# A planned single-core encoder block: steadier operand order, early weights for one output product, and new first and last transfers

## The chip, the cores and the metric

The kernel runs on one core of one Trainium2 chip, in one launch, without collectives. The metric is device time in microseconds. Three runs of the kernel before stand as its time, and one more execution was recorded by the hardware profiler; every row of the trace comes from that one. Engines are named as in the profile: PE (matmul), PEld (its weight loads), DVE, ACT, POOL, and SP, which only issues transfers.

## What is computed

One pre-norm layer on a float32 input of 512 tokens by 1024 channels. An input projection feeds two attention branches, each is gated, and one output projection and a final norm close the layer. Cut to what matters:

```
h = rmsnorm(x, norm_g)
q_lat, c_kv, k_rope, z_a, q_b, k_b, v_b, z_b, q_idx, k_idx, w_idx, gate_a, gate_b = split(h @ w_in)
y_a = chunk_causal_attention(latent q, latent k and v, 8 heads) * silu(z_a)
score = sum over index heads of relu(q_idx . k_idx) * w_idx        # keep the 128 best keys per query
y_b = attention over the kept keys, with a position bias, 8 heads, * silu(z_b)
merged = sigmoid(gate_a) * (y_a @ w_o_a) + sigmoid(gate_b) * (y_b @ w_o_b)
out = rmsnorm(x + merged @ w_out, final_g)
```

## The kernel before

**Precision.** Every operand of a large matmul is split into a rounded high part and the rest (a low part), each in its own 128x512 tile. ACT makes the high part by a copy (L302) or a scaled copy (L311), DVE or POOL subtracts it to get the low part (L328, L330, L339). A product is then three matmuls, high*high, high*low and low*high (`mm3`, recorded at L400). Transposes through the PE are at L417.

**The planner.** Nothing in the program's order is fixed by loops. Each piece of work is a generator that yields one step at a time (a thread, with a priority and a small random nudge), and the class `Flow` plays the whole kernel through at build time: it holds for each engine when it is free, for each buffer when it was last written and read and by whom, and for transfers a modelled queue. Again and again it picks, among the threads' next steps, the one with the smallest key, emits that instruction, and books its modelled duration. So each engine's instruction order is the order of the planner's picks; on the chip each engine then runs its own list strictly in that order and waits where an operand is not there. The pick is this (L199 onwards):

```
s = self.start(t.req, eng)
key = (s + BIAS * t.prio + t.nudge, t.prio)
```

`start` is the first moment at which the engine is free and every operand and buffer is ready. `DRAW` seeds the nudges, so another number gives another order among near-equal steps.

**Buffers.** 73 slots of 128x512 float32 hold nearly everything; four raw buffers of 128x1024 receive weights; eight PSUM banks are shared out by class.

**Start.** `loads` issues on SP, in this order: the first 128 rows of x transposed (s_x, 256 KB), norm_g, the first kv weights, the second rows of x, and so on. `setup` issues the first index-query weights (s_er<-w_qi, 128 KB) from ACT. POOL loads the identity and the latent gains (`setup_pool`, L431). `early_x` splits x (times norm_g) into s_xg tiles: for the first rows ACT makes the high part in three pieces and DVE one low part over all 512 columns. `early_mm` then runs, for each of the eight row blocks k, 6 matmuls of 384 columns for the index queries and 12 of 328 columns for the kv latent, 18 in all.

**Middle.** Projections, the head-by-head latent attention, the index scores, a top-128 search on DVE (L825, L826), the sparse attention, with projections as filler for the PE. The tanh of the gate projection of branch a (s_sig) is written out to scratch in DRAM by SP (`gate`, bias_scratch<-s_sig, eight times) and read back after the projections.

**Output projection.** It is a seven-product scheme on 2x2 blocks; `output` runs products 1, 7, 2, 6, 5, 4, 3 in this order, each 24 matmuls of 512 columns or the same in halves. Their right operands are sums or differences of blocks of w_out. `out_job` loads the blocks into raw buffers from SP, DVE forms the difference (s_wsum), ACT and DVE split it (s_wo). Product 5 needs the difference of two blocks, four tiles of it, and is made near the end like the others.

**End.** `finish` adds the last products to x and squares; `scale_out` sums the three partial squares of a 128-token tile on DVE, takes the power on POOL (L378), scales one half on DVE and one on ACT, and SP sends both halves out. For the last tile the third partial square is made by DVE with its own accumulator (L1768), and one more DVE addition (L328) joins it to the other two.

Of the kernel before, what the change touches and what calls it, by code (L numbers as in the profile page):

```python
# [19 lines left out]
P = 128  # L20
S = 512
# [112 lines left out]
class Flow:  # L134
# [9 lines left out]
    def __init__(self):  # L144
        self.free = {"PE": 0.6, "ACT": 0.6, "DVE": 0.6, "POOL": 0.6, "SP": 0.6}
        self.hw, self.dma = 0.6, 0.0
        self.pbias = -1.0
        self.port = 0.0
        self.threads = []

        self.draw = random.Random(DRAW)

# [6 lines left out]
    def advance(self, t, value):  # L159
        try:  # L160
# [3 lines left out]
            self.threads.remove(t)  # L164

# [17 lines left out]
    def run(self, stop=None):  # L183
        while self.threads:
# [15 lines left out]
            for t in self.threads:  # L200
                if isinstance(t.req, Step):
                    for i, (eng, dur, emit) in enumerate(t.req.options):
                        s = self.start(t.req, eng)
                        key = (s + BIAS * t.prio + t.nudge, t.prio)
# [22 lines left out]
            else:  # L227
# [3 lines left out]
                if step.moves and eng == "ACT":  # L231

                    end += 1.8 + step.moves
# [14 lines left out]
DRAW = 71  # L248
# [4 lines left out]
def tile_block(ctx: ExitStack, tc: tile.TileContext, a: dict, out: bass.AP, bias_dram: bass.AP):  # L253
# [181 lines left out]
    def act_dma(dst, src):  # L435
        step = Step([("ACT", 0.06, lambda: nc.scalar.dma_start(dst.ap, src))], bufs(dst), [])
        step.moves = 4.0 * dst.n * dst.ap.shape[0] / 360000
        return step
# [45 lines left out]
    def setup():  # L484
# [3 lines left out]
        eraw["q", 0] = rq.all.f[:, :256], True  # L488
        yield memset("DVE", zeros.all, 0.0)
# [12 lines left out]
    def setup_pool():  # L502
        yield memset("POOL", mask[0].all, 0.0)
        yield memset("POOL", mask[0][0:64, 64:128], MASK)
        yield Until(lambda: 3 in xt)
        yield from pool_dma(ident.all, a["ident"])
        yield from pool_dma(glat.all, a["g_lat"])
# [20 lines left out]
    def loads():  # L528
        for kp in range(4):
            for kk in range(2):  # L530
                k = 2 * kp + kk
                x = yield slot("x")
                yield dma(x.all.f, a["xT"][k])
                xt[k] = x
                if k == 0:
                    yield dma(normg.all, a["norm_g"])
                if kp == 0:
                    cq, ck = slice(256 * kk, 256 * kk + 256), slice(328 * kk, 328 * kk + 328)
                    if k:
                        rq = yield slot("er")  # L540
                        yield dma(rq.all.f[:, :256], a["w_qi"][kp][:, cq])
                        eraw["q", k] = rq.all.f[:, :256], True
# [11 lines left out]
            if kp == XAT:  # L554
                spawn(x_squares(), PSQ)
                yield is_done("x loads")
# [48 lines left out]
    def split_w(raw, w, dst, key, cls="w", cap=None, release=False, early=False):  # L605
# [3 lines left out]
        yield act(hi[:, :w], raw)  # L609
        step = lo_part(lo[:, :w], raw, hi[:, :w])  # L610
# [5 lines left out]
    first_x = {}  # L616

    def early_x():
        for k in range(NK):
            yield Until(lambda: k in xt)  # L620
            hi = yield slot("xg")
            lo = yield slot("xg")
            if k == 0:

                for piece in PIECES:
                    yield act(hi[:, piece], xt[k].all.f[:, piece], AF.Copy, scale=normg[:, k : k + 1])
                    first_x[piece.start] = hi
                yield stt(lo.all, xt[k].all.f, normg[:, k : k + 1], hi.all.f, ALU.mult, ALU.subtract)
# [4 lines left out]
    def early_w():  # L633
        for k in range(NK):
# [5 lines left out]
            yield from split_w(raw, 328, ewkv, k, "w", WCAP, last, True)  # L640
# [5 lines left out]
    def early_mm():  # L646
# [6 lines left out]
        for i, piece in enumerate(PIECES[:2]):  # L653
            yield Until(lambda: piece.start in first_x)
            for m in range(2):
                yield mm(qi_ps[m][:, piece], [(ewq[0][0][:, m * P : m * P + P], first_x[piece.start][:, piece])], not i, False)
        for k in range(NK):
            yield Until(lambda: k in xg and k in ewq)

            xk = cut(xg[k], SCORED)  # L660
            w = [cut(ewq[k], slice(m * P, m * P + P)) for m in range(2)]
            if k == 0:

                for cw, cx in ((1, 0), (0, 1)):
                    for m in range(2):
                        yield mm(qi_ps[m][:, SCORED], [(w[m][cw], xk[cx])], False, False)
            else:
                for m in range(2):
                    yield mm3(qi_ps[m][:, SCORED], w[m], xk, False, k == NK - 1)
# [4 lines left out]
            for t in range(NT):  # L674
                yield mm3(kv_ps[t][:, :328], cut(xg[k], TOK[t]), cut(ewkv[k], slice(0, 328)), k == 0, k == NK - 1)
# [494 lines left out]
    def gate(name, c, how=proj):  # L1170


        def take(ps):
# [7 lines left out]
            if c in away and name == "w_ga":  # L1181
                yield dma(spilt(c), s.all.f)
# [525 lines left out]
    def out_job(product, c):  # L1708
# [3 lines left out]
        def prep(job):  # L1712
# [11 lines left out]
            else:  # L1724
                for i in range(2):
                    yield Until(lambda: 2 * c + i in sums)
# [13 lines left out]

    xr, fg = {}, {}
# [18 lines left out]
    def finish(t, half, c0, c1, ps, nth, last, keep=False):  # L1760
# [6 lines left out]
        if last:  # L1767
# [292 lines left out]
```

## Time and profile before

| what | value |
|---|---|
| median of 3 runs | 427.27 us (426.54 to 429.5) |
| the profiled execution's own time | 427.16 us |
| its span, first to last instruction | 425.4 us |
| PE, PEld busy | 98%, 86% |
| DVE, ACT, POOL busy | 89%, 62%, 26% |
| granted PE clock, mean | 0.995 |
| HBM read and written | 50.49 MB, 4.21 MB |

The time lies 1.8 us over the span; that is what lies around the recorded instructions. Busy PE time is modelled from pipelined matmuls, so it tells that a matmul was queued, not that the array worked at its peak; spacing between starts tells that.

### The profile page before, as it was taken

How to read it: one execution, taken by the hardware profiler on the slowest of the kernel's cores; microseconds unless marked ns; L12 is line 12 of the kernel's file. 1: busy time of each engine (PE TensorE's matmuls, PEld its weight loads, DVE VectorE, ACT ScalarE, POOL GpSimd, SP SyncE). 2: the span in 40 equal slices, each digit the busy share in tenths (PEclk: the TensorE clock that was granted, in tenths of full speed). 3: DMA queues.
4: the chain of work that ended last, by engine and by line, in shares of the span. 5: the costliest groups of instructions: out<-in, count | busy, mean ns of one | idle time of the engine just before them, and what ended most of it. 6: DMA issues, size and time to landing. Idle time of an engine off the chain costs nothing.

```text
span 425.4 us, 7106 instructions
## 1 busy us (share of the span) xinstructions
PE 415.3 (98%) x2313; PEld 363.9 (86%) x2313; DVE 380.5 (89%) x815; ACT 262.2 (62%) x587; POOL 109.5 (26%) x131
## 2 busy tenths in 40 slices
PE   8999999999999999999999999999999999999993
PEld 6999868889888888888899988998998888888883
DVE  4789899999999999999879888988799757999995
ACT  6778786585573758544864677494598524436624
POOL 1037865455355723121300101000010002210212
PEclk9999999999999999999999999999999999999998
DMA  8973137817255450285243525425523887453705
GB/s 258 394 278 112 52 100 207 230 45 186 82 139 148 127 160 1 79 256 173 63 128 121 171 79 157 146 65 178 146 79 124 266 322 252 143 180 106 242 0 197
DMA packets 30277, 65.89 MB, mean 155 GB/s; under 512 B 4648, under 2 KB 5688, under 8 KB 30240
## 3 DMA queue, kind: packets, MB, share of 16 engines
q1 hardware_dynamic: 29264, 64.08, 48.5%
q0 software_dynamic: 832, 1.22, 0.9%
q8 instruction: 18, 0.29, 0.3%
q14 instruction: 19, 0.16, 0.1%
q10 hardware_dynamic: 144, 0.13, 0.1%
HBM read 50.49 MB, written 4.21 MB: 129 GB/s over the span
## 4 chain that ended last, share of the span: by engine, by line
PE 54%; DVE 30%; DMA 7%; ACT 4%; issue 4%; POOL 0%; POOLq 0%; SPq 0%; DVEq 0%; ACTq 0%
PE ps L400 50%; DVE mask L826 4%; DMA raw<-w_out 4%; DVE sm L825 3%; PE ps L417 2%; DVE sm L1474 2%; DVE s_ph L328 2%; DVE s_mg L328 2%; DVE s_wsum L328 1%; DMA s_sig<-bias_scratch 1%; DVE s_tmp L328 1%; ACT s_p L311 1%; DVE s_pair L328 1%; DVE s_wo L328 1%; DVE s_w L328 1%
## 5 line engine op out<-in xcount | busy, mean ns | idle before, releaser
L400 PE MATMUL ps<-s_h,s_w 128*128 128x512 f32 (+1 forms) x732 | 170.9, 379 | 0.0
L400 PEld LDWEIGHTS ps<-s_h,s_w 128*128 128x128 f32 x732 | 127.8, 189 | 21.8 <-issue 0.3
L302 ACT CAST s_w<-raw 128x512 fp32r<-128x512 f32 (+3 forms) x124 | 71.6, 593 | 17.8 <-DVE raw L328 9.2
L330 POOL TENSOR_TENSOR s_w<-raw,s_w 128x512 fp32r<-128x512 f32 (+2 forms) x35 | 44.7, 1284 | 130.1 <-ACT s_w L302 123.9
L328 DVE TENSOR_TENSOR s_w<-raw,s_w 128x512 fp32r<-128x512 f32 (+2 forms) x89 | 58.7, 670 | 5.3 <-ACT s_w L302 4.7
L400 PE MATMUL ps<-s_ys,s_w 128*128 128x512 f32 x192 | 43.7, 389 | 0.0
L400 PEld LDWEIGHTS ps<-s_ys,s_w 128*128 128x128 f32 x192 | 36.0, 188 | 7.5
L311 ACT ACTIVATE s_p<-s_p,sm 128x384 f32<-128x384 f32 (+3 forms) x54 | 29.2, 559 | 6.8 <-DVE sm L1571 5.6
L400 PE MATMUL ps<-s_wo,s_mg 128*128 128x512 f32 (+1 forms) x156 | 33.0, 373 | 0.0
L400 PE MATMUL ps<-s_w,s_xg 128*128 128x328 f32 (+1 forms) x192 | 32.5, 323 | 0.0
L400 PEld LDWEIGHTS ps<-s_wo,s_mg 128*128 128x128 f32 x156 | 27.6, 188 | 5.2
L400 PEld LDWEIGHTS ps<-s_w,s_xg 128*128 128x128 f32 x192 | 31.4, 188 | 0.0
L328 DVE TENSOR_TENSOR s_ph<-ps,s_ph 128x384 fp32r<-128x384 f32 (+1 forms) x48 | 27.4, 590 | 2.5 <-ACT s_ph L302 2.3
L302 ACT CAST s_ph<-ps 128x384 fp32r<-128x384 f32 (+1 forms) x48 | 23.5, 514 | 5.5 <-PE ps L417 4.2
L311 ACT ACTIVATE s_p<-ps,sm 128x128 f32<-128x128 f32 (+3 forms) x32 | 16.8, 527 | 15.5 <-DVE sm L1474 15.1
L826 DVE MATCH_REPLACE8 mask<-sm,mask 128x384 f32<-128x384 f32 (+2 forms) x48 | 25.8, 540 | 0.0
L825 DVE MAX8 sm<-mask 128x8 f32<-128x384 f32 (+2 forms) x48 | 25.5, 547 | 0.1
L400 PE MATMUL ps<-s_ph,vv 128*128 128x512 f32 (+3 forms) x128 | 24.9, 325 | 0.0
L417 PE MATMUL ps<-ident,s_p 128*128 128x128 f32 x160 | 24.2, 275 | 0.5 <-DVE s_p L358 0.3
L417 PEld LDWEIGHTS ps<-ident,s_p 128*128 128x128 f32 x160 | 18.8, 140 | 4.7 <-ACT s_p L311 1.0
L400 PEld LDWEIGHTS ps<-s_ph,vv 128*128 128x128 f32 x128 | 20.6, 189 | 2.1 <-DVE s_ph L328 0.2
L400 PE MATMUL ps<-s_lat,s_w 128*128 128x512 f32 x78 | 20.5, 398 | 0.0
(197 smaller groups left out, 737.5 us busy)
## 6 DMA issues: line engine op xcount, KB each, us to landing
raw<-w_out SPq DMA_DIRECT2D x18, 512.0 KB, 4.0
s_op<-s_op SPq DMA_DIRECT2D x36, 128.0 KB, 2.3
raw<-w_ga SPq DMA_DIRECT2D x8, 512.0 KB, 4.5
raw<-w_gb SPq DMA_DIRECT2D x8, 512.0 KB, 4.4
raw<-w_o SPq DMA_DIRECT2D x16, 256.0 KB
s_x<-xT SPq DMA_DIRECT2D x8, 256.0 KB, 4.9
s_xn<-x SPq DMA_DIRECT2D x8, 256.0 KB, 5.7
bias_scratch<-s_sig SPq DMA_DIRECT2D x8, 256.0 KB, 2.5
```

The source lines that it names most:

```text
L302: nc.scalar.copy(dst.ap, src.ap)
L311: nc.scalar.activation(dst.ap, src.ap, func, **kw)
L328: opts.append(("DVE", 0.07 + 0.00104 * x.n, lambda: nc.vector.tensor_tensor(dst.ap, x.ap, y.ap, op=op)))
L330: opts.append(("POOL", 0.15 + 0.0021 * x.n, lambda: nc.gpsimd.tensor_tensor(dst.ap, x.ap, y.ap, op=op)))
L400: nc.tensor.matmul(ps.ap, l.ap, r.ap, start=start and i == 0, stop=stop and i == len(pairs) - 1, skip_group_check=more)
L417: nc.tensor.transpose(d.ap, s.ap, ident.tile)
L825: yield Step([("DVE", t, lambda: nc.vector.max(m8.tile, work.tile))], [m8], [work])
L826: yield Step([("DVE", t, lambda: nc.vector.match_replace(work.tile, m8.tile, work.tile, MARK))], [work], [m8])
L1474: yield Step([("DVE", 0.07 + 0.00104 * n, lambda: nc.vector.tensor_reduce(mx.tile[:, 1:2], ps.tile[:, :n], op=ALU.max, axis=AX.X, negate=T ...
```

## The change

In the planner, the key of a step for PE or SP now adds a demand: each operand or buffer that DVE, ACT or POOL last touched should have been ready for 2.0 us (PE) or 1.0 us (SP). A step that is not settled so may still be picked, but behind others. The modelled cost of transfers issued by ACT changes, and the seed.

```
+    def settled(self, step, eng, start):
+        s = start
+        for b in (*step.ins, *step.outs):
+            for e, t in ((b.by, b.w), *b.reads.items()):
+                if e != eng and e in SETTLE[eng]:
+                    s = max(s, t + self.lat(e, eng) + SETTLE[eng][e])
+        return s
...
-                        key = (s + BIAS * t.prio + t.nudge, t.prio)
+                        key = ((self.settled(t.req, eng, s) if eng in SETTLE and s < math.inf else s) + BIAS * t.prio + t.nudge, t.prio)
...
-DRAW = 71
+DRAW = 37
+SETTLE = {'PE': {'DVE': 2.0, 'ACT': 2.0, 'POOL': 2.0}, 'SP': {'DVE': 1.0, 'ACT': 1.0, 'POOL': 1.0}}
```

At the start, ACT issues three transfers: the first index-query weights, the lower half of the first x rows, and the second index-query weights; SP loads the upper half of x first. The low part of the first x rows is made in three pieces, each right behind its high part, and the kv matmuls of the first row block go high weights first, from the last token tile to the first. The identity and the latent gains go to SP, behind the transposed x.

```
         yield act_dma(rq.all.f[:, :256], a["w_qi"][0][:, :256])
...
+        yield act_dma(x0[1].all.f[:, LO], a["xT"][0][:, LO])
...
+        yield act_dma(rq.all.f[:, :256], a["w_qi"][0][:, 256:512])
...
-        yield from pool_dma(ident.all, a["ident"])
-        yield from pool_dma(glat.all, a["g_lat"])
...
+                    yield dma(x.all.f[:, HI], a["xT"][0][:, HI])
...
+                yield dma(ident.all, a["ident"])
+                yield dma(glat.all, a["g_lat"])
...
+                for t in (3, 2, 1, 0):
+                    i = (2, 1, 0, 0)[t]
+                    yield Until(lambda: i in first_low)
+                    x = cut(first_x[i], TOK[t])
+                    yield mm(kv_ps[t][:, wide], [(x[0], first_kv[0][:, wide]), (x[1], first_kv[0][:, wide])], True, False)
```

In the middle, the eight gate tiles are written out by ACT's queue instead of SP's:

```
             if c in away and name == "w_ga":
-                yield dma(spilt(c), s.all.f)
+                yield act_move(spilt(c), s.all.f)
```

Product 5's right operand is made once branch b's head 1 is done, from blocks that POOL's queue loads (eight transfers of 256 KB), and POOL's queue writes both parts to a scratch tensor in DRAM (eight more). SP reads them back (eight) once product 6's operands are there. Product 5 leaves the list of `out_job`s, with its four transfers of 512 KB on SP.

```
+    def make():
+        yield is_done(("b", 1))
+        for product in MADE:
...
+            for k in range(4):
+                raw = yield slot("raw")
+                yield from pool_dma(raw.all, w_block(h, g, k))
+                if product == 5:
+                    other = yield slot("raw")
+                    yield from pool_dma(other.all, w_block(0, 0, k))
+                    yield tt(raw.all, raw.all, other.all, ALU.subtract)
+                    put(other)
...
+                yield act(hi.all, raw.all)
+                yield lo_part(lo.all, raw.all, hi.all, ("DVE",))
...
+                for part, t in enumerate((hi, lo)):
+                    yield from pool_dma_out(made(product, k, part), t.all.f)
...
+    def fetch_made():
...
+                yield is_done(("made", product, k), "projections")
+                yield Until(lambda: first is None or first in right or first in used)
...
+                    t = yield slot("wo", 32)
+                    yield dma(t.all.f, made(product, k, part))
...
+MADE = (5,)
+PMAKE = 16
```

At the end, for the last tile the sum of the first two partial squares is the starting value of the third one's accumulator, so the addition behind it goes; and the second half of that tile is sent by ACT's own queue.

```
-                junk.tile[:, : r.n], r.ap, r.ap, op0=ALU.mult, op1=ALU.add, scale=1.0, scalar=0.0,
-                accum_out=ssf[t].tile[:, nth : nth + 1]))], [junk, ssf[t]], bufs(r))
+                junk.tile[:, : r.n], r.ap, r.ap, op0=ALU.mult, op1=ALU.add, scale=1.0, scalar=s.tile[:, 0:1],
+                accum_out=s.tile[:, 1:2]))], [junk, s], [r.buf, s])
...
+            if t == 1 and half:
+                yield Step([("ACT", 0.06, lambda: nc.scalar.dma_start(dst, x.ap))], [], bufs(x))
+            else:
+                yield dma(dst, x)
```

More of the change, by code (lines that the diff above doesn't have):

```diff
@@ L623, in early_x @@
             if k == 0:
[L625 to L628, printed above, removed]
+                for i, piece in enumerate(PIECES):
+                    if i == 1:
+                        yield Until(lambda: 0 in xt)
+                    if i == 2:
+                        yield Until(lambda: first_kv)
+                    x = x0[i > 0].all.f[:, piece]
+                    part = Buf(hi.tile, "xg"), Buf(lo.tile, "xg")
+                    yield act(part[0][:, piece], x, AF.Copy, scale=normg[:, 0:1])
+                    first_x[i] = part
+                    yield stt(part[1][:, piece], x, normg[:, 0:1], part[0][:, piece].f, ALU.mult, ALU.subtract)
+                    first_low.add(i)
+                for whole_, of in zip((hi, lo), part):
+                    whole_.w, whole_.by, whole_.written = of.w, of.by, True
             else:
```

116 lines of the change are left out of this document (83 added, 33 removed).

## The prediction

> **What bounds the kernel now.** I read the page, then the stages, then PE's waits, then both ends in order of time.
>
> ```profile
> PE 415.3 (98%) x2313; PEld 363.9 (86%) x2313; DVE 380.5 (89%) x815; ACT 262.2 (62%) x587; POOL 109.5 (26%) x131
> ...
> 40.00:60.00 20.00, 19.03 (x105) 16.22 (x104) 17.91 (x28) 16.32 (x36) 14.54 (x18) 1.00 0.26 79
> 160.00:180.00 20.00, 19.74 (x102) 16.30 (x101) 19.77 (x39) 14.11 (x33) 5.27 (x6) 1.00 0.15 41
> 200.00:220.00 20.00, 19.75 (x130) 17.60 (x129) 16.82 (x38) 14.30 (x33) 4.22 (x3) 1.00 0.26 60
> 340.00:360.00 20.00, 20.00 (x90) 16.55 (x89) 12.52 (x20) 7.08 (x13) 3.17 (x2) 1.00 0.84 293
> ```
>
> In a stage's row PE's busy time stands behind the length. At 340 us the PE runs at full pace, 90 matmuls of 512 columns in 20.00 us, 0.222 us each, at a granted clock of 1.00 (third number from the end). Between 20 and 400 us only the three other stages lose more than 0.1 us. So the PE's own list is the path, and since the change leaves its matmuls as they are, it can gain in three places: before the PE is in step, where it waits, and behind its last matmul. The waits, each with what ran just ahead:
>
> ```profile
> 55.99 0.60 PE L417 MATMUL ps<-ident,s_latraw 128*128 128x128 f32 x4
> 56.35 0.65 PE L803 MATMUL ps<-s_qs,s_qs 96*128 96x512 f32 x2
> 57.97 0.31 PE L852 MATMUL ps<-s_oh,rbs 64*8 64x320 f32 x1 [0.97 <-DVE mask L339]
> ...
> 166.38 0.63 PE L400 MATMUL ps<-s_h,s_w 128*128 128x512 f32 x2
> 167.26 0.70 PE L417 MATMUL ps<-ident,s_p 128*128 128x128 f32 x3 [0.26 <-DVE s_p L358]
> ...
> 212.09 0.38 PE L417 MATMUL ps<-ident,s_p 128*128 128x128 f32 x2
> 212.73 0.44 PE L417 MATMUL ps<-ident,s_p 128*128 128x128 f32 x2 [0.25 <-ACT s_p L311]
> ```
>
> Ends are modelled, so I price a wait by starts. At 56.35 a matmul of 512 and one of 384 columns are worth 0.39 us at the pace above, and the next start comes 1.62 us later: 1.2 us lost. At 166.38 two of 512 are worth 0.44 us of 0.88: 0.4 lost. At 212.09 two transposes (four took 0.36 us at 55.99) are worth 0.2 us of 0.64: 0.4 lost. Together 2.0 us, all behind an operand or bank that DVE or ACT had only just finished.
>
> **The change part by part.** *The start.*
>
> ```profile
> 3.00:4.00 1.00, 1.00 (x6) 0.70 (x5) 0.00 (x0) 0.00 (x0) 0.00 (x0) 1.00 1.00 279
> 4.00:5.00 1.00, 0.52 (x4) 0.09 (x1) 0.43 (x1) 0.96 (x3) 0.00 (x0) 1.00 0.84 153
> 6.00:7.00 1.00, 0.79 (x5) 0.72 (x5) 0.64 (x2) 0.00 (x0) 0.00 (x0) 1.00 1.03 363
> ...
> 2.08 0.56 POOL L431 DMA_DIRECT2D glat<-g_lat  x1
> 4.04 0.40 ACT L302 CAST s_w<-s_er 128x256 fp32r<-128x256 f32 x1 [1.38 <-DMA s_er<-w_qi]
> 4.36 1.09 ACT L311 ACTIVATE s_xg<-s_x,normg 128x256 fp32r<-128x256 f32 x3
> 5.43 0.47 ACT L302 CAST s_w<-s_er 128x328 fp32r<-128x328 f32 x1
> 7.05 0.72 ACT L311 ACTIVATE s_xg<-s_x,normg 128x512 fp32r<-128x512 f32 x1 [1.15 <-DMA s_x<-xT]
> 7.81 0.75 DVE L339 SCALAR_TENSOR_TENSOR s_xg<-s_x,normg,s_xg 128x512 fp32r<-128x512 f32 x1 [1.17 <-ACT s_xg L311]
> 8.52 1.40 PE L400 MATMUL ps<-s_xg,s_w 128*128 128x384 f32 x6
> 11.57 1.21 PE L400 MATMUL ps<-s_xg,s_w 128*128 128x384 f32 x6
> 14.40 1.20 PE L400 MATMUL ps<-s_xg,s_w 128*128 128x384 f32 x6
> ...
> glat<-g_lat POOLq DMA_DIRECT2D x1, 2.5 KB, 4.8
> ```
>
> A row block of 18 matmuls takes 2.83 us (11.57 to 14.40). The second block takes 3.05 (8.52 to 11.57), so it starts in effect at 8.74, because its low part leaves DVE only at 7.81 + 0.75 = 8.56. That chain hangs on the second rows of x, for which ACT waits until 7.05. So a faster first block alone gains nothing: what counts is when those rows land, and when ACT is free for them.
>
> The landing: SP issues them in the same fourth place as before. But the identity and the gains, which POOL issued from 1.32 us on and of which the gains' 2.5 KB took 4.8 us to land, leave this stretch. It moves 279 and 153 GB/s between 3 and 5 us, against 363 at 6 us; at 363 the same bytes pass (84 + 210) / 363 = 0.8 us sooner, so the rows land between 6.25 and 7.05. ACT: its list ahead of them becomes three pieces of the first rows (1.09 in all), two casts of 256 columns (0.40 each) and two of 328 (0.47 each), 2.83 us. It can begin when the first data land: 128 KB less stand ahead, 0.46 us at 279 GB/s, so about 3.6 for 4.04. The list ends at 6.4, the high part at 7.15 for 7.77: 0.6 us sooner. If the data land no sooner it is 0.2, and if the rows of x land no sooner it is nothing; at best 0.8. I take 0.6, as the stalled stretch is plainly there. The first block (from about 4.6 for 4.91, 2.83 of work and one wait of up to 0.6 for the second piece behind a cast) ends by 8.1 and hides below it. Both moved loads now stand on SP between x transposed and x, where the block stream has the PE covered, and cost nothing unless that cover goes: then two issues, 0.9 us.
>
> The row at 4 us shows engines 84% busy and slow. [...]
>
> *The order.* The planner now wants each of PE's operands 2.0 us old. I counted in both programs' instruction lists, pricing PE at 0.222 us per 512 columns, how much PE work lies between the last touch by ACT, DVE or POOL and the matmul that needs it. Before, 127 of 491 such handovers have under 2 us and 38 under 0.9, the three waits among them; after, 20 of 467 and 4. Three of those 4 are in the first block. So the 2.0 us go; between nothing and 2.0, I take all of it. What is late next is the fourth: the norm's transposes move from inside the last block to behind it, and the bank they fill is wanted 0.5 us of PE work later by the latent products, with a copy by ACT in between.
>
> ```profile
> L311 ACT ACTIVATE s_sig<-ps 128x512 f32<-128x512 f32 x10 | 6.0, 597 | 14.6 <-PE ps L400 11.9 <-POOL s_w L330 2.8
> ```
>
> The nearest row is this read of a bank, 0.6 us: 0.1 us is uncovered, and with two handovers up to 0.6. I take +0.3.
>
> *Early weights, and queues.*
>
> ```profile
> 220.00:290.00 70.00, 70.00 (x482) 65.10 (x482) 61.21 (x137) 47.60 (x108) 3.12 (x3) 1.00 0.44 136
> 360.00:410.00 50.00, 50.00 (x233) 41.88 (x232) 49.43 (x87) 22.83 (x43) 7.80 (x6) 1.00 0.46 150
> ...
> ropec<-ropec POOLq DMA_DIRECT2D x1, 256.0 KB, 6.7
> 0.73 0.41 ACTq L436 DMA_DIRECT2D s_er<-w_qi  x1
> SPq L427 <- DVE s_w L328: 111.4, 37, 15.0
> ```
>
> Four subtractions, four casts and four low parts move from the stage at 360 us to that at 220. DVE gets some 5.4 us there (eight times 0.68) on top of 61.21 in 70.00: it fits. Leaving 360 us, where DVE is busy 49.43 of 50.00, brings nothing, since the PE is busy 50.00 of 50.00 there: I cost it at nothing. Sixteen POOL transfers at the 6.7 us of the one of this size are far ahead of their use, and POOL has 3.12 us of work in those 70. The eight reads come in on SP about 10 us of PE work before product 5 uses each; six would have to land late together to show. The eight gate tiles cost ACT up to 0.41 us of issue each, 3.3 us on an engine that is 62% busy; behind each stand casts that feed PE, with 2 us of margin now. Cost nothing; 3.3 us if no cover held.
>
> *The end.*
>
> ```profile
> 420.09 0.08 DVE L1768 DVE_READ_ACCUMULATOR2_ANT ssf<- 128x1 f32 x1
> 420.21 0.16 DVE L328 TENSOR_TENSOR sm<-sm,ssf 128x1 f32<-128x1 f32 x1
> 420.45 0.66 POOL L378 TENSOR_TENSOR sm<-sm,neghalf 128x1 f32<-128x1 f32 x1 [1.32 <-DVE sm L328]
> 421.15 0.72 ACT L311 ACTIVATE s_rg<-s_rg,sm 128x512 f32<-128x512 f32 x1 [1.27 <-POOL sm L378]
> 422.09 0.38 SPq L427 DMA_DIRECT2D out<-s_rg  x1
> ```
>
> Without the addition POOL follows the accumulator's end (420.17) by the 0.08 us with which it follows DVE now: 0.2 us. ACT ends the last half at 421.87 and can issue it there, where SP issued at 422.09: 0.2 us more. I take -0.4, between -0.2 and -0.5.
>
> *The sum*: -0.6 - 2.0 + 0.3 - 0.4 = -2.7 us on 427.16 (425.4 of span and 1.8 around it), 424.5; the profiled execution lies 0.1 under the median of the runs, so 424.4 stays my number, 0.7% off.
>
> **The rivals.** *More than the waits goes.* All 876 thousand columns at the block's pace (2.83 us for its 6240) are 397.5 us, and 188 transposes cost some 0.05 more each than their columns: 407 of the 413.7 from 4.91 to the last matmul's end near 418.6. Start and waits explain 3; the other 4 are short hitches without a row of their own. If they are handovers just missed, half may go: -0.8 - 2.0 + 0.1 - 0.5 - 2.0 = -5.2, 422.0. For it: the count falls to a sixth. Against: the fillers are cut as finely as before, so switching costs stay.
>
> *The order does not do what it says.* The planner's margins hold by its own durations. If the three waits come back elsewhere, only the ends are left: -0.6 - 0.4 + 0.3, 426.5. For it: DVE is busy 89%, and any slip passes down its list. Against: 2 us is more than any wait shown.
>
> *ACT blocks on its transfers*, and the kernel is slower. In the build each gate tile's issue also waits for the transfer eight places earlier among those of SP and ACT. SP stands 111.4 us in 37 waits on DVE alone, 3.0 us each, 15.0 at worst. If that transfer has not landed, ACT stops in its list, with casts for PE and bank reads behind it. It decides once the stop exceeds the 2 us of margin: six stops of 3.0 plus a landing of some 2.5 us less 2 give +21 at worst, and half of them 10: 435. Against it: the earlier transfer stands at least 5.9 us of PE work ahead in the list.
>
> **How the numbers follow.** Forecast 0.50; more than the waits 0.24; the order does nothing 0.17; ACT blocks 0.09. The likeliest gives 424.4. The range is 421.6 to 428.6: the first reaches the best case, the second the case without an order's gain and with part of a stop; beyond it 0.15 is left. A measurement tells 1% (4.3 us, so 423.0 and 431.5) from no change. Faster by more comes from the first rival alone: 0.24. Slower by more needs ACT's stops: 0.08. The rest, 0.68, is within 1%.
>
> **What would show it.** Right: the second block in effect near 8.1; no wait of PE over 0.2 us after 30 us; POOL's last power 0.2 us behind the accumulator's read; the last transfer issued by ACT. Wrong: a PE wait over 1 us anywhere after 30 us; ACT idle behind its own issue of a gate tile; product 5 waiting for its weights; or spacing that changes where no wait is named.

## The result

The changed kernel is slower: ratio to the kernel before 1.0045, 95% interval 1.0029 to 1.0060 (medians 429.78 and 428.02 us, 20 runs each), and in a second series 1.0025, 1.0003 to 1.0048. The forecast of 0.7% faster was wrong in its sign. Both programs spread by some 4 us from run to run, so a single profile shows one case of several. The profiled execution of the changed kernel took 430.3 us with a span of 428.5, 3.1 more than the span before.

The page's first part and, behind it, PE's waits (in total, times, longest), changed kernel:

```profile
PE 418.0 (98%) x2313; PEld 367.1 (86%) x2313; DVE 376.6 (88%) x804; ACT 263.9 (62%) x591; POOL 123.6 (29%) x153
```

```profile
PE ps L853 <- DMA s_qs<-s_th: 1.5, 1, 1.5
PE ps L524 <- DVE neghalf L472: 1.1, 1, 1.1
PE ps L411 <- ACT s_xg L322: 0.7, 1, 0.7
PE ps L411 <- ACT s_w L313: 0.4, 1, 0.4
PE ps L411 <- ACT s_rbc L313: 0.2, 1, 0.2
```

Of the three waits that the prediction priced, none is left: no row names the bias table's mask, and no row names `s_p`. In their place stands one wait of 1.5 us for a transfer. The last row is a wait at 33.1 us, behind the norm's transposes; the other three belong to the first 7 us.

**The start.** First the stages of the changed kernel, then 7 to 8 us of the kernel before, then PE of the changed one in order of time:

```profile
6.00:7.00 1.00, 0.59 (x3) 0.59 (x3) 0.92 (x3) 1.00 (x5) 0.00 (x0) 1.00 0.93 327
7.00:8.00 1.00, 1.00 (x5) 1.00 (x5) 0.89 (x3) 1.00 (x3) 0.00 (x0) 1.00 1.05 380
```

```profile
7.00:8.00 1.00, 1.00 (x9) 1.00 (x8) 0.19 (x1) 0.95 (x3) 0.00 (x0) 1.00 1.01 313
```

```profile
8.28 3.48 PE L411 MATMUL ps<-s_w,s_xg 128*128 128x328 f32 x12
11.56 1.71 PE L411 MATMUL ps<-s_xg,s_w 128*128 128x384 f32 x6
13.11 1.95 PE L411 MATMUL ps<-s_w,s_xg 128*128 128x328 f32 x12
14.90 1.20 PE L411 MATMUL ps<-s_xg,s_w 128*128 128x384 f32 x6
```

From 7 to 8 us the PE is busy all the time in both kernels, with 5 matmuls here and 9 before. The twelve of 328 columns take 11.56 - 8.28 = 3.28 us, 0.273 each; the same twelve in the next block take 14.90 - 13.11 = 1.79, 0.149 each. So PE runs at about half its pace until about 12.5 us. The column of the granted clock reads 1.00 all along, because it counts the time ahead of the first recorded change of the clock as granted in full. The packed trace holds these changes: the first one, to 1.00, is at 12.66 us here and at 5.11 in the kernel before. The third block begins at 14.90, against 11.57 before: 3.3 us lost. The chain of waits between 3 and 16 us says what held the first block:

```profile
1.63 3.93 DMA s_er<-w_kvl
...
5.59 0.46 ACT s_w L313
6.05 0.31 ACT s_xg L322
...
6.41 9.69 PE ps L411 x42
```

The first rows of `w_kvl` land at 5.56. ACT casts them ahead of the second piece of x, which stands ready behind, and PE is idle until 6.41.

**The middle and the end.** In order of time, PE's last products before, then those of the changed kernel with its end:

```profile
412.77 5.80 PE L400 MATMUL ps<-s_wo,qhi 128*128 128x512 f32 x36
```

```profile
416.26 5.80 PE L411 MATMUL ps<-s_wo,qhi 128*128 128x512 f32 x36
423.27 0.08 DVE L1862 DVE_READ_ACCUMULATOR2_ANT sm<- 128x1 f32 x1
423.43 0.67 POOL L389 TENSOR_TENSOR sm<-sm,neghalf 128x1 f32<-128x1 f32 x1 [1.19 <-DVE sm L1862]
424.13 0.72 ACT L322 ACTIVATE s_rg<-s_rg,sm 128x512 f32<-128x512 f32 x1 [0.93 <-POOL sm L389]
424.88 0.34 ACTq L1906 DMA_DIRECT2D out<-s_rg  x1
```

The last matmul ends at 418.57 before and at 422.06 after. From the third block to that end it is 407.00 before and 422.06 - 14.90 = 407.16 after: the new order gave nothing. From that end to the span's it is 6.83 before and 6.48 after. The sum: 3.33 + 0.16 - 0.35 = 3.14, the 3.1 us between the spans.

### The profile page after: what moved, and what is told of

Its sections match the earlier page's. It is cut to its first block, busy times and chain, and to the rows that moved or that the text cites. A ratio compares the mean times of both kernels' runs of the same rounds, so it can differ in the third digit from the quotient of the medians.

```text
span 428.5 us, 7155 instructions
## 1 busy us (share of the span) xinstructions
PE 418.0 (98%) x2313; PEld 367.1 (86%) x2313; DVE 376.6 (88%) x804; ACT 263.9 (62%) x591; POOL 123.6 (29%) x153
## 4 chain that ended last, share of the span: by engine, by line
PE 82%; DVE 6%; ACT 4%; DMA 4%; issue 2%; POOL 0%; SPq 0%; POOLq 0%; ACTq 0%; DVEq 0%
PE ps L411 74%; PE ps L428 4%; ACT s_p L322 2%; DVE s_w L339 1%; PE ps L1542 1%; PE ps L1543 1%; ACT s_w L313 1%; PE ps L1541 1%; DMA s_op<-s_op 1%; DMA s_er<-w_kvl 1%; DMA s_qs<-s_th 1%; DMA raw<-w_kb 1%; DVE raw L339 1%; DVE s_tmp L339 1%; PE ps L853 1%
## 5 line engine op out<-in xcount | busy, mean ns | idle before, releaser
L341 POOL TENSOR_TENSOR s_w<-raw,s_w 128x512 fp32r<-128x512 f32 (+2 forms) x40 | 50.4, 1261 | 61.1 <-ACT s_w L313 39.0
L339 DVE TENSOR_TENSOR s_w<-raw,s_w 128x512 fp32r<-128x512 f32 (+2 forms) x84 | 55.9, 677 | 4.4 <-ACT s_w L313 4.1
L411 PE MATMUL ps<-s_w,s_xg 128*128 128x328 f32 (+1 forms) x192 | 34.3, 334 | 0.2 <-ACT s_rbc L313 0.2
L411 PEld LDWEIGHTS ps<-s_w,s_xg 128*128 128x128 f32 x192 | 32.9, 197 | 0.5 <-ACT s_rbc L313 0.5
L322 ACT ACTIVATE s_p<-s_p,sm 128x256 f32<-128x256 f32 (+3 forms) x56 | 28.8, 540 | 7.0 <-DVE sm L1621 6.3
L411 PE MATMUL ps<-s_ph,vv 128*128 128x512 f32 (+3 forms) x128 | 27.1, 324 | 0.0
L875 DVE MAX8 sm<-mask 128x8 f32<-128x256 f32 (+2 forms) x48 | 25.4, 548 | 0.6 <-POOL mask L472 0.2
L876 DVE MATCH_REPLACE8 mask<-sm,mask 128x256 f32<-128x256 f32 (+2 forms) x48 | 25.9, 541 | 0.0
L428 PE MATMUL ps<-ident,s_p 128*128 128x128 f32 x160 | 23.3, 272 | 0.0
```

Of the source, the lines that this page charges most:

```text
L322: nc.scalar.activation(dst.ap, src.ap, func, **kw)
L339: opts.append(("DVE", 0.07 + 0.00104 * x.n, lambda: nc.vector.tensor_tensor(dst.ap, x.ap, y.ap, op=op)))
L341: opts.append(("POOL", 0.15 + 0.0021 * x.n, lambda: nc.gpsimd.tensor_tensor(dst.ap, x.ap, y.ap, op=op)))
L411: nc.tensor.matmul(ps.ap, l.ap, r.ap, start=start and i == 0, stop=stop and i == len(pairs) - 1, skip_group_check=more)
L428: nc.tensor.transpose(d.ap, s.ap, ident.tile)
L875: yield Step([("DVE", t, lambda: nc.vector.max(m8.tile, work.tile))], [m8], [work])
```

## The experiments

Three questions: is the slow start what made it slower, where did the order's gain go, and what are the early weights worth.

### The start

Four kernels at first. `fill` adds matmuls of zeros that nothing reads, `oldstart` takes the start of before back, `gap` leaves zeros out of the kernel before.

```diff
 # fill (constants 2 and 4), behind the warm-up and behind the first piece
+        fill(EXTRA)
         put(ps)
...
+            if i == 0:
+                fill(BETWEEN)
 # gap, in the kernel before
-        for _ in range(NWARM):
-            yield pe(WARM, [ps.all], [zeros.all], lambda: nc.tensor.matmul(
+        for i in range(NWARM):
+            yield pe(WARM, [ps.all], [zeros.all], lambda: i > 6 or nc.tensor.matmul(
```

> The changed kernel with six more matmuls of zeros that nothing reads, two behind the fifteen of the warm-up and four between the first and the second piece of the first rows, all else in the same order. Theory, the clock: PE stood idle from 5.5 to 6.4 us, and its pace stayed at half until 12.5 us, which cost 2.9 us. With the gaps filled the pace is full by 8 us and the time falls to 427.5 (426.8 to 428.2) from 429.8. Rival, late data: the loss is the wait for the second piece and the late transfer of the score operands at 87.7 us, and the half pace does not hang on the idle time: 429.8 (429.3 to 430.3), pace half until some 12 us.

Measured: 430.36 us, ratio 1.0042 (1.0017 to 1.0068). Its one profile shows the full pace from 5.4 us on and a span of 426.3, as the theory has it, but that was the second lowest of its 12 runs (428.1 to 432.4), and the median moved not at all. A miss, and with that spread no proof against the clock either.

> The changed kernel with the start of the kernel before: first rows of x in one transfer, identity and gains on POOL's queue, first block as before; the rest is planned anew with the same margins. Theory, the clock: PE has no idle stretch near 6 us, pace full by 7 us, time 427.3 (426.5 to 428.2). Rival, the order: margins of 2 us push transfers and lose what they gain in the middle, and the start costs little: 429.5 (428.8 to 430.2).

Measured: 434.12, 1.0135 (1.0104 to 1.0166). Neither: the rest was planned anew and has waits of 0.2 to 1.5 us at seven places behind 40 us. Nor is its start that of before: ACT casts the first index-query weights behind the pieces of x, PE stands idle for 1.2 us ahead of its first product, the clock first changes at 10.33 us and the third block begins at 13.88. What a new plan draws is larger than what was to be measured, so the next kernels leave the plan alone and change only what is issued.

> The kernel before with seven of the fifteen matmuls of zeros left out of its warm-up (the last eight), nothing else moved. Theory, the clock: PE is idle from 2.6 to 4.9 us and its pace stays at half for some 3 to 6 us longer, so 1.5 to 3 us are lost: 430.2 (429.3 to 431.2) beside 428.0. Rival: the zeros do no work, so leaving some out costs nothing: 428.0 (427.5 to 428.5).

Measured: 428.00, 0.9987 (0.9973 to 1.0001), with a profile that shows the late pace:

```profile
4.86 2.50 PE L400 MATMUL ps<-s_xg,s_w 128*128 128x256 f32 x8 [2.14 <-ACT s_xg L311]
7.16 3.16 PE L400 MATMUL ps<-s_w,s_xg 128*128 128x328 f32 x12
10.15 1.20 PE L400 MATMUL ps<-s_xg,s_w 128*128 128x384 f32 x6
11.20 1.95 PE L400 MATMUL ps<-s_w,s_xg 128*128 128x328 f32 x12
```

The twelve take 2.99 us instead of 1.79, and the third block starts at 12.98 for 11.57: the half pace is there without any new order, in a profile with 2.14 us of idle PE before its first product (the clock's first change is at 9.80 us). But the time is no worse than that of the kernel before: either the other runs had the pace early, or what is lost there is made up elsewhere, and one profile cannot tell. The expectation of 2 us was a miss.

Next, 33 zeros instead of 15 in both kernels, so that the start is the same in both.

```diff
                 ps.tile[:, :256], z[:, :P], z, start=True, stop=True))
+        for _ in range(18):
+            nc.tensor.matmul(ps.tile[:, :256], z[:, :P], z, start=True, stop=True)
         put(ps)
```

> The kernel before with 33 matmuls of zeros in place of 15, nothing else moved, so that PE is never idle from 1.05 us to its first real product and the pace is at full when that begins, whatever moment the clock changes. First real product between 6.3 and 8.1 us; the first two blocks then take 2.83 us each, so the third starts near 12.9 (12.0 to 13.8) against 11.6+2.8 = 14.4 for the fourth in the profile before: about 1.3 us later than in that profile, 426.7 of span. Theory, the moment of the clock's change is what spreads the runs: time 428.5, and the runs lie within 2 us instead of 4. Rival, the spread is in the weights' transfers: the runs still spread over 4 us.

> The changed kernel with the same 33 matmuls of zeros, nothing else moved. It takes the start out of the comparison with the run above. Theory, the changed start is what made the kernel slower (the block ran at half pace until 12.5 us): here the rest is left, 0.15 lost in the middle and 0.4 gained at the end, so 428.2 (427.5 to 428.8), within 0.5 us of the run above. Rival, the new order loses by itself through late transfers: 1.5 to 2 us above the run above, 430.2.

Measured: 428.32, 1.0022 (1.0003 to 1.0041) for the kernel before; 427.77, 1.0007 (0.9986 to 1.0028) for the changed one. The third blocks start at 11.85 and 12.13. With the start padded the changed kernel is no longer the slower one, as the theory said: the excess of 1.0045 falls to 1.0007, while the kernel before loses a little. The runs still spread over 3 us, so the pace's moment is not all of the spread.

With 24 zeros in both (9 more in place of 18), and, in `swap`, with two instructions of ACT exchanged and 15 zeros:

```diff
 # swap: the cast of w_kvl's first rows is held back ...
-        yield act(hi[:, :w], raw)
+        step = act(hi[:, :w], raw)
+        if cast == []:
+            (eng, dur, emit), = step.options
+            step.options = [(eng, dur, lambda: held.append(emit))]
+        yield step
 # ... and issued behind the scaling of the second piece
+                    if i == 1:
+                        held.pop()()
```

> The changed kernel with 24 matmuls of zeros in place of 15, nothing else moved. They end by 6.2 us at the latest, so the wait for the second piece at 6.4 is covered and PE's busy stretch is whole from 1.05 us on. Theory: the clock is at full by 7.2 us in every run, the first block ends 1 us earlier than with 33 zeros on the average, and the time is 427.3 (426.7 to 427.9), 2 us below the changed kernel. Rival, what the 33 zeros bought was late data that had landed, not the clock: 429.0.

> The kernel before with 24 matmuls of zeros in place of 15, nothing else moved. With 15, PE is idle for 0.7 us ahead of the first product alone, so less hangs on it than in the changed kernel: 427.8 (427.2 to 428.4) beside 428.0. By the theory that the changed order and end are 0.5 us better once the start is the same, it lies 0.5 above the run above.

> The changed kernel with two instructions of ACT exchanged: the cast of w_kvl's first rows now stands behind the scaling of the second piece of x, nothing else moved. In the changed profile ACT stood 0.76 us for that cast's data at 5.59 with the second piece queued behind it, and PE was idle from 5.5 to 6.4. Theory, ACT's order makes the idle stretch: the scaling runs at 4.9, PE's second piece at 5.6, the clock reaches full more often by 7 us, and 1 us or more goes: 428.7 (427.9 to 429.3). Rival, the second piece's data land only near 6 us: nothing changes, 429.8.

Measured: 24 zeros 429.18, 1.0021 (1.0000 to 1.0042), changed; 428.19, 0.9998 (0.9983 to 1.0014), before. Here the changed kernel is 1 us above the other instead of 0.5 below, and 1.9 us above what was expected. Both pairs of padded starts together leave the two kernels level to within a microsecond, not the changed one ahead. The exchange of ACT's two instructions: 429.15, 1.0025 (1.0006 to 1.0044). Its profile shows where the wait goes:

```profile
4.54 0.40 ACT L322 ACTIVATE s_xg<-s_x,normg 128x128 fp32r<-128x128 f32 x1
5.81 0.77 ACT L313 CAST s_w<-s_er 128x328 fp32r<-128x328 f32 x2 [0.88 <-DMA s_er<-w_kvl]
...
6.31 0.50 DVE L339 TENSOR_TENSOR s_w<-s_er,s_w 128x328 fp32r<-128x328 f32 x1 [1.12 <-ACT s_w L313]
6.73 0.34 DVE L350 SCALAR_TENSOR_TENSOR s_xg<-s_x,normg,s_xg 128x128 fp32r<-128x128 f32 x1
...
7.13 0.62 PE L411 MATMUL ps<-s_xg,s_w 128*128 128x384 f32 x2 [0.90 <-DVE s_xg L350]
```

The second piece is scaled at 4.54 and no longer at 5.96, so its data had been there. Then DVE stands in the same place: the low part of `w_kvl` is ahead of the low part of that piece, and PE waits at 7.13. What both wait for is the transfer of `w_kvl`. Under the old start it lands no sooner (in `tail` its cast waited until 5.82), but there its cast stands behind the pieces of x; the new start put it ahead of them on two engines.

Last, the changed kernel unaltered, for a second profile:

> The changed kernel once more, unaltered, for a second profile. Three profiles of its start, this kernel's first and two others with the same start, began the third row block at 14.90, 13.85 and 11.25 us, with PE's pace at half until 12.5, 10.4 and no later than 5.9. Theory, the moment at which the pace doubles is free of the program and shifts all that follows: the third block starts between 11.2 and 14.9, and the span is 428.5 less what it starts earlier, to within 1.2 us for the transfers' waits. Rival, the start is always as slow as in the first profile: 14.9 again.

```profile
6.38 2.08 PE L411 MATMUL ps<-s_xg,s_w 128*128 128x128 f32 x6 [0.82 <-ACT s_xg L322]
8.26 2.59 PE L411 MATMUL ps<-s_w,s_xg 128*128 128x328 f32 x12
10.69 1.20 PE L411 MATMUL ps<-s_xg,s_w 128*128 128x384 f32 x6
...
13.51 0.68 PE L411 MATMUL ps<-s_xg,s_w 128*128 128x384 f32 x3
```

Measured: 429.63, 1.0025 (1.0003 to 1.0048). The same program changes its pace at 9.66 us in this run, at 12.66 in the first. Seven profiles have the unaltered new start: these two and, below, `settle_dma`, `gather_act`, `no_early_weights`, `no_margin` and `no_margin_71`. They began the third block at 14.90, 13.51, 13.85, 12.41, 11.25, 14.85 and 15.56 us, 13.8 on the average, and the clock's first change stands at 12.66, 9.66, 10.49, 4.85, 5.54, 12.05 and 13.30. Three of the old start (the kernel before, `tail` and `before_margin`) began it at 11.57, 11.48 and 11.36, with the change at 5.11, 4.05 and 5.50. The new start costs 2.3 us on the average, with a standard deviation of 1.5 between profiles. From the first product of the second piece to the third block it takes 5.63 and 5.66 us in the two profiles with an early change and 7.13 to 8.49 in the other five. So 1.6 of the 2.3 us are pace, and the rest comes from how late the second piece begins.

What the traces show of the pace: about half of it at first (0.273 us a matmul of 328 columns against 0.149 in the first profile), a moment of change that moves between runs of one program (12.66 and 9.66 us), and behind it a stretch at 1.00 of 413.013 us in that profile and of 416.426 in the kernel before, whose difference, 3.413, goes into them 121 and 122 times. What sets the moment they do not show. That a gap of PE ahead of the first change can cost more than its length was an estimate of mine, and no run's time shows it: `gap`, with 2.14 us of idle PE and the change at 9.80, took no longer than the kernel before. One gap behind the change left the pace as it was: in `gather_act` PE stood idle for 1.36 us after the change at 4.85 and kept its pace.

A fast start is also paid for later. Behind the norm's transposes PE waits for `s_rbc`, a copy that ACT makes behind the cast of a small bias table (`rb`), and that table lands between 29.3 and 31.1 us. Two kernels introduced below reached their third block first in this order, `no_early_weights` at 11.25 us and `best` at 11.46. In their profiles PE lost 2.5 and 1.4 us at this place, against 0.2 to 0.3 in the other profiles of this order. ACT, PE and a stage of `no_early_weights`:

```profile
31.10 0.20 ACT L313 CAST rbs<-rb 64x8 fp32r<-64x8 f32 x1 [1.70 <-DMA rb<-rel_bias]
31.21 0.57 ACT L313 COPY s_rbc<-ps 128x512 f32<-128x512 f32 x1
31.83 8.43 PE L411 MATMUL ps<-s_w,s_xg 128*128 128x384 f32 x38 [2.50 <-ACT s_rbc L313]
33.00:36.00 3.00, 3.00 (x11) 3.00 (x11) 3.00 (x9) 2.71 (x8) 1.78 (x3) 0.50 0.68 221
```

Behind that wait the clock falls to 0.50 for 3.4 us. No run takes this wait away alone, so its price in the medians is not shown. The mean clock of each run suggests that such falls are not rare: profiles without one ahead of the last matmul have 0.995 to 0.998, while 12 of the changed kernel's 32 runs have 0.992 or less, against 1 of 36 with 24 or 33 zeros and none of 133 of the kernel before. Where those 12 runs lost the clock is not shown, and they are not clearly slower than the other 20.

### The order

The changed kernel with margins for SP's transfers too, then without margins under both draws, and the kernel before with margins alone:

```diff
-SETTLE = {'PE': {'DVE': 2.0, 'ACT': 2.0, 'POOL': 2.0}, ...
+SETTLE = {'PE': {'DVE': 2.0, 'ACT': 2.0, 'POOL': 2.0, 'SP': 2.0}, ...   # settle_dma
+SETTLE = {}                                                             # no_margin; no_margin_71 with DRAW = 71
```

> The changed kernel whose planner also wants the operands that SP's transfers bring 2.0 us old, before a product of PE prefers them; the start is the same up to 56 us, what follows is planned anew. Theory: the wait of 1.66 us for the score operands at 87.7 us came because the margin knows ACT, DVE and POOL alone, so it goes: 428.3 (427.3 to 429.3). Rival: another plan is another draw, its waits come back elsewhere: 430 to 434, as with the old start.

> The changed kernel without the margins (the planner's key is the earliest start again), planned anew. Theory, margins trade waits for ACT and DVE for waits for SP's transfers, which they do not know: PE's waits for ACT and DVE behind 40 us come back (1.5 to 2.5 us in sum), its waits for transfers near 85 and 275 us fall under 0.5, and the time is within 1 us of the changed kernel's 429.8. Rival, the margins are worth the forecast 2 us: 431.8. Rival, any new plan of this program is a draw and most are worse than the one that was kept: 432 to 436.

> As the run above with the planner's draw of the kernel before (71 for 37), a second plan without margins. Theory as above: 429.8 within 1 us, waits for ACT and DVE and not for transfers. Rival, the draw decides: the two plans without margins lie more than 2 us apart.

> The kernel before with the margins and the draw of 37 alone, planned anew; start, end and weights as before. Theory: waits for ACT and DVE behind 40 us fall under 0.6 in sum, waits for transfers come to 1 us or more, the time lies at 428.0 within 1 us. Rival, forecast: 426.3. Rival, the draw decides: 431 or more.

Measured: 429.23, 1.0041 (1.0020 to 1.0063); 436.52, 1.0177 (1.0139 to 1.0215); 431.28, 1.0043 (1.0019 to 1.0068); 437.38, 1.0203 (1.0166 to 1.0240). The longest of PE's waits behind 40 us in `no_margin`, then in `no_margin_71`, then in `before_margin`:

```profile
PE ps L411 <- DVE s_w L339: 1.9, 1, 1.9
PE ps L411 <- DVE s_ph L339: 1.3, 1, 1.3
PE ps L853 <- DMA s_qs<-s_th: 1.0, 1, 1.0
```

```profile
PE ps L428 <- DVE s_p L369: 1.0, 1, 1.0
PE ps L411 <- ACT s_pair L313: 0.7, 1, 0.7
```

```profile
PE ps L410 <- ACT s_wo L312: 5.7, 1, 5.7
```

Without margins waits for DVE and ACT are back in both plans, as expected. But margins alone do not keep them away: behind 40 us `before_margin` has 7.3 us of them in sum (under 0.6 was expected), `oldstart` 3.8 and `settle_dma` 1.4, all with margins, against 1.5 in the kernel before and none in the changed one. And the theory that margins trade them for waits on transfers falls: `no_margin` has the wait for the score's gathers too, and `settle_dma` lost it (PE's list names no transfer) and waits elsewhere. The two plans without margins lie 5 us apart. Which waits a plan has is to a large part its draw.

The gathers themselves, in the changed kernel in order of time:

```profile
76.52 1.18 SPq L438 DMA_DIRECT2D s_qs<-s_th  x2
...
83.36 1.14 SPq L438 DMA_DIRECT2D s_qs<-s_th  x2
...
85.81 0.39 PE L411 MATMUL ps<-s_h,s_w 128*128 128x512 f32 x1
87.70 0.36 PE L853 MATMUL ps<-s_qs,s_qs 96*128 96x256 f32 x1 [1.50 <-DMA s_qs<-s_th]
```

SP issues the last head's pair with eight other transfers between it and the pair before. `best` has 24 zeros, the exchange on ACT, and this pair issued by SP right behind the pair before; `gather_act` gives the pair to ACT's queue instead, without other edits, and `longwarm_gather` does so with 33 zeros.

```diff
                 q = yield slot("qs")
+                if 4 * m + j == NH - 1:
+                    for c, t in ((1, tl), (2, th)):
+                        # gather_act; in best the same on nc.sync
+                        nc.scalar.dma_start(q.tile.bitcast(F32)[32 * c : 32 * c + 32, SCORED],
+                                            t.tile.bitcast(F32)[32 * j : 32 * j + 32, SCORED])
```

> The changed kernel with 24 matmuls of zeros, the two instructions of ACT exchanged, and SP's two gathers of the last score head issued right behind those of the head before it, in place of seven transfers later; nothing else moved. PE waited 0.9 to 1.7 us for those gathers near 85 us in four profiles of this order. Theory: that wait falls under 0.2 and is not paid later, as PE sets the pace behind it: 426.3 (425.7 to 427.2), under both kernels. Rival, what is pulled ahead delays the attention's gathers behind it on SP, and DVE, busy for all of this stretch, takes the place of the wait: 427.3.

> The changed kernel with the last score head's two gathers issued by ACT's queue at about 77.5 us in place of SP's at 83.4, nothing else moved. In the three profiles of the changed kernel's plan that were least disturbed PE waited 1.66, 1.87 and 1.05 us for them, while SP issued nine transfers in a row and ACT was idle for 1.9 us between 80 and 85. Theory: the wait goes without a new one, and 1.2 us stay gained at the end: 428.5 (427.8 to 429.1) beside 429.7. Rival, as when SP issued them earlier (431.7 with the other two edits): the attention's gathers behind them come late and PE waits there: 429.7 or more.

> The changed kernel with both mends: 33 matmuls of zeros, so that the pace is full when the first product begins, and the last score head's gathers by ACT's queue; order of PE as in the changed kernel. Theory: what is left of the change is PE without waits for engines behind 40 us and the shorter end: 426.6 (426.0 to 427.3), 1.2 below the run with 33 zeros alone (427.8) and clear of the kernel before (428.4). Rival, run-to-run landings at 235 and 275 us eat it: 427.8.

Measured: `best` 431.73, 1.0074 (1.0046 to 1.0101). The rival was right and more: PE has no wait for the gathers, but 2.0 us at the attention's first product behind them, beside the 1.4 us at 31 us and 1.2 us for a transfer at 277 us:

```profile
87.50 0.30 PE L1556 MATMUL ps<-s_op,qhi 100*128 100x128 f32 x1 [1.95 <-issue]
```

The row names no releaser. But SP issues the gathers of `kpe` from 82.64 us on here and from 84.54 on in the changed kernel, whose third block started 3.4 us later: they come 1.5 us later for their place. SP's list is full there, and what was pulled ahead pushed these back. `gather_act`: 428.79, 1.0026 (1.0002 to 1.0050), with a span of 425.3 in its profile; the wait for the gathers is gone and has left this one behind:

```profile
PE ps L1548 <- DMA s_op<-kpel: 0.7, 1, 0.7
```

`longwarm_gather`: 427.49, 0.9981 (0.9959 to 1.0003). From the third block to the last matmul's end it is 406.4 and 406.0 in these two, against 406.2 to 408.7 (407.5 on the average) in six profiles of the changed plan and 406.8 to 408.2 (407.2) in five of the plan before. So that wait took back some 1.3 us by the profiles; the timed runs point the same way with 33 zeros (1.0007 to 0.9981) and are too wide to say it without. `longwarm_gather` has the lowest ratio of all runs, but its interval reaches 1: no version here is clearly faster than the kernel before.

### Early weights and the end

```diff
-MADE = (5,)
+MADE = ()      # no_early_weights
```

> The changed kernel without the early weights (product 5's weights are made in the last stage again); PE's list is the same up to its 1,400th matmul near 235 us. Theory, early weights cost and bring nothing: 429.8 (429.2 to 430.4). Rival, the sixteen transfers of POOL and the split work slow the stage from 220 to 290 us: 428.8. Rival, the last stage needs them early: 431.

Measured: 436.20, 1.0197 (1.0152 to 1.0243), worse than any of the three. The runs go from 431.79 to 437.92, and the profile is of the slowest; 2.5 us of its loss are the wait at 31 us. PE's longest wait in `no_early_weights`, and stages of `before_margin`, which has margins without early weights as well:

```profile
PE ps L411 <- ACT s_wo L313: 3.0, 1, 3.0
```

```profile
405.00:409.00 4.00, 4.00 (x28) 3.65 (x27) 4.00 (x4) 0.48 (x1) 2.99 (x2) 1.00 0.00 0
409.00:415.00 6.00, 0.92 (x5) 0.41 (x3) 6.00 (x13) 1.69 (x7) 0.00 (x0) 1.00 0.00 1
416.00:420.00 4.00, 4.00 (x10) 2.89 (x10) 0.28 (x1) 0.00 (x0) 0.00 (x0) 0.50 0.00 0
```

DVE is busy for all of 409 to 415 while PE is busy 0.92 of 6 us: the last products' weights are not made in time. Behind that the granted clock is 0.50, and PE needs 0.4 us a matmul until 421.9. Both plans with margins and without early weights wait for `s_wo` there; none of the five plans with early weights does. With margins, the early weights carry the last stage.

> The kernel before with the new end alone (the last sum of squares starts from the other two, the last half goes out by ACT's queue); order and all else as before. Theory: the stretch from the last matmul's end to the span's end falls from 6.8 to 6.4 us, time 427.6 (427.3 to 427.9) beside 428.0. Rival: the last transfer's landing sets the end and ACT's issue brings nothing, so only the addition's 0.2 goes: 427.8.

Measured: 428.26, 0.9988 (0.9969 to 1.0007), in line with 0.4 us and not clear of none. The stretch behind the last matmul was 6.45 to 7.63 us in four profiles of the old end (6.8 on the average, but two of them under 6.5), 6.63 in `tail`, and 6.48 or 6.49 in each of the changed plan's: 0.2 to 0.4 shorter on the average.

## Why the prediction was wrong

- **The start, -0.6: this step failed, and with it the sign.** "2.83 of work" was the block's price at full pace, which the first blocks do not have in every run; I took that pace for given, though no row that I quoted showed it between 4.9 and 8 us. The measured price is +3.3 in the profile and +2.3 on the average of profiles, 1.6 of it pace; with it in place of -0.6 the sum of -2.7 becomes +0.2. Two inputs were off as well. The wait behind a cast, "up to 0.6", was 0.4 to 1.5 in the seven profiles, and the first data did not come at 3.6 but at 4.0, as before. ACT's first instruction on loaded data starts at 4.02 us, against 4.04 before, though ACT's queue issued three transfers in place of one: between 3 and 4 us 272 GB/s were moved, against 279 before, and more only from 4 to 5, 272 against 153.
- **The order, -2.0 + 0.3: failed in its size.** The three waits did go in this plan, though the other plans with margins do not show that it was the margins that took them. The norm's transposes cost 0.4 at 33.1 (0.92 us between starts for three matmuls of 384 columns, worth 0.52), near the 0.3 of the sum, and more where the start is faster. But the count of handovers took ACT, DVE and POOL as the last to touch an operand and left out SP's transfers. The wait of 1.7 for a pair of gathers stood where the count saw nothing. The rival with its gain gone through waits elsewhere (426.5) described this term best.
- **Early weights at nothing: wrong, though not in the sum.** I costed their leaving the last stage at nothing since PE was busy there in the kernel before. That cover held for the old order alone; in plans with margins the stage without them lost 3.0 and 5.7 us of waiting, and in both the clock was at half for 6.8 us behind it.
- **The end, -0.4: right** in the pair of profiles (6.83 to 6.48); on the averages 0.2 to 0.4.
- **ACT blocking on its transfers** did not come: behind the issue of a gate tile ACT stands 0.4 us at most, four times, little more than the 0.33 of the issue itself.
- **The rival of short hitches** rests on 0.05 us more for each transpose than for its columns. The quoted row (four in 0.36 us) gives 0.03, so its 4 us without a row of their own were too few.

Sum by what was measured: 2.3 (start) + 0.3 (407.2 to 407.5 in the middle) - 0.4 = 2.2 us, beside 1.9 and 1.1 from the two ratios. That the start's loss is mostly pace rests on profiles: `gather_act` began its third block 0.8 late at full pace, from late data, and `fill` and `gap`, which were to move the pace, moved the time less than their profiles say. So its cause stays open in part. Also open is the rest of the spread: with the start padded the runs still differ by up to 4 us, and waits that go back to transfers, at 85, 235 and 275 us, change between profiles of one plan.

## What to carry to other kernels

Price the first microseconds from the spacing of matmuls in the trace (0.273 us here), not from the steady pace (0.149), and look whether an edit opens a gap of PE there; then look for the next place that is tied to a transfer's landing, where a faster start is lost again (2.5 us at 31 us in `no_early_weights`). A second profile tells whether what you read is the program or the run. Counting margins before a product must take transfers in as well as engines (PE waited 1.5 us for a pair of gathers), and look what a transfer pulled ahead on a full queue pushes back: in `best` the gathers of `kpe` came 1.5 us later for their place, and ACT's queue was the better one here. In a planned kernel test an edit with the order frozen, since new plans moved the time by up to 2%.

## What was not expected of the hardware

The pace doubled anywhere from 4.85 to 13.30 us under starts of the same code, with the clock's column at 1.00 throughout. Later the clock fell to 0.50 behind waits much shorter than those near the end: for 3.4 us behind 2.5 us of idle PE in `no_early_weights` (at 31.8) and behind 1.9 us in `no_margin` (at 331.8), while 2.0 us at 87.5 in `best` left it at 1.00. And transfers of one order land at different times: two tiles of `w_gb`, issued by SP at 219.4 us in the kernel before and in `tail`, let DVE go on without a wait in the first profile and held it in the second, where PE then lost 0.9 us at 235.6:

```profile
226.77 0.69 DVE L328 TENSOR_TENSOR s_wsum<-raw 128x512 f32<-128x512 f32 x1 [1.36 <-DMA raw<-w_gb]
235.62 1.70 PE L400 MATMUL ps<-s_h,s_w 128*128 128x256 f32 x12 [0.70 <-ACT s_pair L302]
```
